# An encoder layer with 16 experts on one core: the Fourier transform and the ranks issued in steps, and gate and up in matmuls of 512 and 256 columns

## The chip, the core and the metric

The kernel runs on one core of a Trainium2 chip. A core has TensorE (matmuls; in the profile PE, its weight loads PEld), VectorE (DVE), ScalarE (ACT), GpSimd (POOL) and SyncE (SP, which here only issues DMAs). The metric is the device time of one execution in microseconds (us); the time before is the median of 3 runs.

## The reference, cut to what matters

One layer on a sequence of 2048 positions with 1024 channels, float32:

- `h = RMSNorm(x)`, `p = h @ w_in`, split into 512 columns each of `lru_x`, `lru_gate` and `fourier`.
- A = GeLU(lru_gate) * (forward + backward gated linear recurrence of a depthwise convolution of lru_x).
- B = the real part of a 2-D FFT over positions and channels of the `fourier` columns, in 4 groups of 128 channels.
- `x = x + concat[A, B] @ w_out`.
- A mixture of 16 experts: a softmax router gives every position a score for every expert; each expert takes its 256 best positions, gathers them, computes `silu(xin @ w_gate) * (xin @ w_up)` with 2048 hidden units, multiplies by `w_down`, scales by the score and adds the rows back. A last RMSNorm gives the output.

Every matmul of float32 operands is made of three in the format fp32r: each operand is split into a high part (a rounded copy, made on ScalarE) and a low part (the rest, made on VectorE), and the products high x high, high x low and low x high are added in PSUM. The helper `split` (L82, its instructions at L85 and L86) makes the parts, the helper `mm3` (L76, instructions L78, L79, L80) the three matmuls.

## The kernel before, in words

The instructions of one engine run in the order in which a planner has put them. The planner follows the order of the program and its own estimate of when each instruction could start; `issue_after` and `high_priority` move single ones. Tiles of one name share a fixed number of buffers; a buffer is given to the next tile when the last reader of the old one is done.

**Before the experts.** `pre_moe` (L176 to L497) computes the projections. `first_x` and `four` make lru_x for eight blocks of 256 positions. `lru(b)` (L280) computes the recurrence for 128 channels: convolution, 48 gate matmuls into PSUM tiles `gt`, sigmoids, tanh, exp, square, sqrt on ScalarE, and two scans of 2048 elements on VectorE (L328, L330). `mixin` and `stage1` make the Fourier columns and the first step of the transform, and store it in DRAM (`v_d`). `gates` makes lru_gate and stores it in DRAM (`gt_d`). lru(0) comes before the mixin loop, lru(1) in its block 4, lru(2) and lru(3) in blocks 0 and 4 of the gates loop (L369, L383). Then comes the transform (L477 to L491): 16 steps (i, gr), where `load_v` brings the columns back from DRAM and splits them into tiles `vl` (6 buffers), with the twiddle tiles `tw` (4), `stage2` multiplies them (PSUM `mm`) and splits the result into `xfh`/`xfl`, and `chans` of the step before multiplies by cosine and sine (PSUM `gt`) and adds into `Yt` (L470 to L475). In the same loop `gelu(i)` (L389) loads 2048 gate values per partition, applies GeLU and multiplies u, once in each i, and `load_wo` (L406) brings four of the eight row blocks of w_out; its low part is made on GpSimd (L412). The other four blocks are loaded after the transform.

**w_out and router.** `w_out_phase` (L503) handles 16 tiles of 128 positions: `prep(n)` splits u and Yt of a tile, `mix(n)` multiplies by w_out, first the four blocks of Yt, then the four of u, and the router follows some tiles later.

**Routing.** `routing` (L715): `first` finds the threshold of expert 0, `ranks` and `digits` turn scores above the threshold into slot numbers. For the other 15 experts `others` (L896) does the same in 30 steps of `search` on VectorE, followed at once by `ranks` (whose matmuls at L838 wait for its counts at L834 and L835), two transposes and `digits`. These steps are handed out by `aside` (L1162) while expert 0 is computed, three before and three after each `gate_up`.

**Experts.** `moe` (L911) loops over 16 experts of 8 chunks. A chunk holds 256 hidden units. `load(e, c)` fetches gate, up and down weights (1 MB each) into `raw`, and splits them into `wh` and `wl`, 4 buffers each. `gate_up(e, c)` (L1031) multiplies the gate weights, then the up weights: for each of two blocks `s` of 128 hidden units and each of 8 blocks `k` of channels one `mm3` with 256 columns, 96 matmuls in all. Then SiLU, product and split into `hh`. `down` of the chunk before follows, 24 matmuls of 512 columns. PSUM: three banks `mm`, four banks `dn`, one bank `gt`. In the program's order PE therefore runs gate_up(c), down(c-1), gate_up(c+1), down(c).

For the next expert `slots(e + 1)` is issued after `down` in chunk 3 (chunk 5 in expert 0): `pick` (L918) prepares `dv` on GpSimd, runs 16 small matmuls (L929), two more at L934 and one at L945 in the PSUM bank `gt`, VectorE derives the row numbers `iq` (L951), and GpSimd issues 8 gathers (L970). `xin(e + 1)`, issued in chunk 5 (chunk 7 in expert 0), transposes the gathered rows on VectorE (L994) and splits them into `xh` and `xl`.

Of the kernel before, what the change touches and what calls it, by code (L numbers as in the profile page):

```python
# [9 lines left out]
F32 = mybir.dt.float32  # L10
# [4 lines left out]
OP = mybir.AluOpType  # L15
# [131 lines left out]
def pre_moe(tc, nc, a, g, ctx):  # L147
# [115 lines left out]
    pg = tc.alloc_tile_pool(name="pg", bufs=1, reuse_waits="tile")  # L263
    with tc.tile_pool(name="pl", bufs=1, reuse_waits="tile") as pl:
        kk = pl.tile([P, 2, P], F32R, name="kk")
        split(nc, g.cc[:, 0:P], kk[:, 0], kk[:, 1])
# [13 lines left out]
        def lru(b):  # L280
# [11 lines left out]
            sg = [pg.tile([P, S], F32, name="rf", bufs=1), pg.tile([P, S], F32, name="if", bufs=1), t8("rb"), t8("ib")]  # L292
# [89 lines left out]
        for c in range(8):  # L382
            if c in (0, 4):  # L383
                load_gm(2 + c // 4)
                lru(2 + c // 4)
            if c + 1 < 8:
                pre[c + 1] = next_x(c + 1)
            gates(c, w, pre.pop(c))
    def gelu(b):  # L389
        gl = pg.tile([P, S], F32, name=("rf", "if")[b % 2], bufs=1)  # L390
        nc.sync.dma_start(gl.rearrange("p (c t) -> p c t", c=8), gt_d[:, b // 2, :, b % 2 * 256:b % 2 * 256 + 256].rearrange("c p t -> p c t"))
        with tc.issue_after(g.last_sqrt.ins):
            nc.scalar.activation(gl, gl, AF.Gelu_apprx_tanh)
        uv = u[:, b, 2:2 + S].rearrange("p (b t i) -> p t b i", t=16, i=8)
        V.tensor_tensor(uv, uv, gl.rearrange("p (t b i) -> p t b i", t=16, i=8), OP.mult)
# [10 lines left out]
    def load_wo(k, pool):  # L406
# [12 lines left out]
    def load_v(i):  # L419
        vv, tt = {}, {}  # L420
        with soon():
            for k2 in sets[i]:
# [4 lines left out]
                tt[k2] = tw
                for v in ([0] if k2 == 0 else [15] if k2 == 8 else [2 * k2 - 1, 2 * k2]):
                    raw = pf.tile([P, DL], F32, name="vraw", bufs=2)
                    nc.sync.dma_start(raw, g.v_d[v])  # L430
# [48 lines left out]
    for i in range(4):  # L479
        for gr in range(4):  # L480
# [12 lines left out]
    pg.release()  # L493
# [9 lines left out]
def w_out_phase(tc, nc, a, g):  # L503
# [26 lines left out]
    with tc.tile_pool(name="po", bufs=1, reuse_waits="tile") as po:  # L530
        wr = po.tile([P, KD, E], F32, name="wr")
# [685 lines left out]
```

## Time and profile before

| what | us |
|---|---|
| median of 3 runs (2901.05 to 2906.13) | 2905.11 |
| the profiled execution, its own time | 2904.78 |
| its span, first to last instruction | 2902.8 |
| TensorE busy in the span | 2817.6 (97%) |
| first gate_up matmul of expert 0 | 684.7 |
| first gate_up matmul of expert 1 | 825.3 |

Times in rows are microseconds from the start of the span. Matmuls are pipelined: the length that a row gives to one is its passage, and the distance between the starts of two is what it costs. PEclk is the granted TensorE clock, 1.00 for 2.4 GHz and 0.50 for 1.2 GHz.

### The profile page before, as it was taken

Reading aid. Unit: us, or ns where it says so; the run is one execution under the profiler, and the core shown is the slowest. Engines: PE = TensorE matmul, PEld = TensorE weight load, DVE = VectorE, ACT = ScalarE, POOL = GpSimd, SP = SyncE. Lnnn points to the kernel's source line nnn. Section 1 sums busy time; section 2 is a strip of 40 time slices with the busy share of each in tenths; the row PEclk is TensorE's granted clock in tenths of the full one; section 3 lists DMA queues with packets and bytes.
Section 4 is the critical chain, followed back from the end, with each engine's and each line's share of the span. In section 5 each row is a group of like instructions: output and inputs, shape, how many; then the busy total and the mean of one; then the engine's idle time right before and its main releaser. Section 6 shows DMA issues by size and latency. Waiting matters only on the chain.

```text
span 2902.8 us, 45048 instructions
## 1 busy us (share of the span) xinstructions
PE 2817.6 (97%) x19215; PEld 2596.3 (89%) x19215; DVE 1763.4 (61%) x2064; ACT 1282.1 (44%) x1341; POOL 412.3 (14%) x362
## 2 busy tenths in 40 slices
PE   8999979997999999999999999999999999999998
PEld 8878867776899999999999999999999999999997
DVE  7664775558865565555555555656555555565565
ACT  5584653333344334434343434434444434443465
POOL 3111122011021111111102020211111111111110
PEclk9999989997999999999999999999999999999999
DMA  8546454446565656565656566565656565656585
GB/s 298 198 162 204 170 190 146 155 149 227 174 206 202 200 192 203 197 197 202 202 192 203 198 193 210 187 212 204 202 191 203 197 198 200 203 191 202 200 290 221
DMA packets 129001, 578.45 MB, mean 199 GB/s; under 512 B 18176, under 2 KB 36000, under 8 KB 79648
## 3 DMA queue, kind: packets, MB, share of 16 engines
q1 hardware_dynamic: 108368, 507.37, 50.3%
q0 software_dynamic: 20288, 68.17, 8.2%
q8 instruction: 150, 2.46, 0.3%
q14 instruction: 51, 0.42, 0.0%
q10 hardware_dynamic: 144, 0.03, 0.0%
HBM read 508.40 MB, written 67.11 MB: 198 GB/s over the span
## 4 chain that ended last, share of the span: by engine, by line
PE 73%; DVE 2%; issue 0%; DMA 0%; ACT 0%; POOLq 0%; ACTq 0%
PE mm L78 17%; PE mm L79 16%; PE mm L80 16%; PE dn L78 8%; PE dn L79 8%; PE dn L80 8%; DVE wl L86 1%; DVE junk L793 0%; PE gt L929 0%; DVE cq L796 0%; DMA rows<-h_d,ix 0%; DVE cr L794 0%; DVE cs L795 0%; DMA out<-rows,ix 0%; DVE dl L826 0%
## 5 line engine op out<-in xcount | busy, mean ns | idle before, releaser
L85 ACT CAST wh<-raw 128x2048 fp32r<-128x2048 f32 x384 | 730.3, 1906 | 1190.2 <-PE mm L79 759.1
L86 DVE TENSOR_TENSOR wl<-raw,wh 128x2048 fp32r<-128x2048 f32 x384 | 888.8, 2318 | 562.4 <-ACT wh L85 561.3
L78 PE MATMUL mm<-xh,wh 128*128 128x256 f32 x4096 | 1163.0, 284 | 0.1
L79 PE MATMUL mm<-xl,wh 128*128 128x256 f32 x4096 | 1161.8, 284 | 0.3 <-DVE xl L86 0.3
L80 PE MATMUL mm<-xh,wl 128*128 128x256 f32 x4096 | 1160.3, 283 | 0.0
L78 PEld LDWEIGHTS mm<-xh,wh 128*128 128x128 f32 x4096 | 786.8, 192 | 7.5 <-ACT xh L85 0.3
L79 PEld LDWEIGHTS mm<-xl,wh 128*128 128x128 f32 x4096 | 786.8, 192 | 5.8 <-DVE xl L86 0.5
L80 PEld LDWEIGHTS mm<-xh,wl 128*128 128x128 f32 x4096 | 786.9, 192 | 4.6 <-issue 4.6
L78 PE MATMUL dn<-wh,hh 128*128 128x512 f32 x1024 | 400.0, 391 | 0.0
L79 PE MATMUL dn<-wl,hh 128*128 128x512 f32 x1024 | 399.9, 391 | 0.0
L80 PE MATMUL dn<-wh,hh 128*128 128x512 f32 x1024 | 398.3, 389 | 0.0
L80 PEld LDWEIGHTS dn<-wh,hh 128*128 128x128 f32 x1024 | 192.3, 188 | 40.9
L1072 POOL DMA_INDIRECT acc<-y,ix x30 | 70.9, 2362 | 1103.0 <-DVE y L1071 1020.9
L78 PEld LDWEIGHTS dn<-wh,hh 128*128 128x128 f32 x1024 | 192.8, 188 | 36.7
L79 PEld LDWEIGHTS dn<-wl,hh 128*128 128x128 f32 x1024 | 192.8, 188 | 35.1
L970 POOL DMA_INDIRECT rows<-h_d,iq x120 | 137.1, 1143 | 588.6 <-DVE iq L951 545.7
L1044 DVE TENSOR_TENSOR sg<-sg,mm 128x512 f32<-128x512 f32 x128 | 87.1, 681 | 151.4 <-PE mm L80 146.2
L78 PE MATMUL mm<-xx,w 128*128 128x256 f32 x512 | 147.2, 289 | 8.4 <-ACT xx L192 6.3
L994 DVE STREAM_TRANSPOSE z<-rows 128x256 f32<-128x256 f32 x120 | 74.3, 655 | 124.4 <-DMA rows<-h_d,iq 112.3
L79 PE MATMUL mm<-xx,w 128*128 128x256 f32 x512 | 146.5, 288 | 0.1
L80 PE MATMUL mm<-xx,w 128*128 128x256 f32 x512 | 145.3, 288 | 0.2 <-DVE w L89 0.2
L85 ACT CAST hh<-sg 128x512 fp32r<-128x512 f32 x128 | 78.6, 614 | 74.6 <-DVE sg L1044 74.5
(378 smaller groups left out, 2922.4 us busy)
## 6 DMA issues: line engine op xcount, KB each, us to landing
raw<-w_gate SPq DMA_DIRECT2D x128, 1024.0 KB, 4.9
raw<-w_up SPq DMA_DIRECT2D x128, 1024.0 KB, 4.8
raw<-w_down SPq DMA_DIRECT2D x128, 1024.0 KB, 4.9
xx<-x_d SPq DMA_DIRECT2D x64, 512.0 KB, 4.5
x_d<-xx SPq DMA_DIRECT2D x32, 512.0 KB, 3.8
xr<-xT SPq DMA_DIRECT2D x32, 256.0 KB, 4.0
xrow<-x SPq DMA_DIRECT2D x16, 512.0 KB, 3.7
acc<-x POOLq DMA_DIRECT2D x16, 512.0 KB
```

The lines of the kernel that those rows point to most:

```text
L78: nc.tensor.matmul(out, sh, mh, start=first, stop=False, skip_group_check=shared)
L79: nc.tensor.matmul(out, sh, ml, start=False, stop=False, skip_group_check=shared)
L80: return nc.tensor.matmul(out, sl, mh, start=False, stop=last, skip_group_check=shared)
L85: nc.scalar.copy(hi, raw)
L86: return nc.vector.tensor_tensor(lo, raw, hi.bitcast(F32), OP.subtract)
L970: nc.gpsimd.indirect_dma_start(out=r[:, o * 256:(o + 1) * 256], out_offset=None, in_=g.h_d.rearrange("t (q c) -> (t q) c", q=4), in_offset ...
L994: V.transpose(out=xt[:, :, 32 * o:32 * o + 32], in_=comb(rows[o // 4][:, o % 4 * 256:(o % 4 + 1) * 256]))
L1044: turn[e, c] = V.tensor_tensor(sg, sg, pu, OP.mult)
L1072: nc.gpsimd.indirect_dma_start(out=g.acc, out_offset=bass.IndirectOffsetOnAxis(ap=idx[h][:, :1], axis=0), in_=y, in_offset=None, compute_o ...
```

## The change

- The recurrences move forward: lru(1) and lru(2) to blocks 3 and 7 of the mixin loop, lru(3) to block 3 of the gates loop.
- `gelu` is cut in 16 pieces of 512 elements; its loads go from the SP queue to the GpSimd queue, 12 pieces are issued ahead of the transform, 4 within it. More buffers for `vraw`, `vl` (8) and `tw` (5); tiles are named at the head of each pool, which fixes their place in memory.
- The low part of w_out is made on VectorE instead of GpSimd. The blocks 0 to 3 (of u) are loaded during the transform, 4 to 7 (of Yt) after it. For the first two tiles the u half of `mix` is issued ahead of everything that reads Yt, into four PSUM banks `mm` that are kept until the Yt half has been added.
- `ranks` becomes a generator: after the counts, three steps pass before its matmuls, and three more before the transposes. `slots(1)` moves from chunk 5 to chunk 6 of expert 0.
- PSUM in the experts: four banks `mm`, four `dn`; `pick` takes one of the four `mm` banks.
- `xh` and `xl` become one tile, [k, high or low, 256]. From expert 1 on, for each block s and each of gate and up: eight matmuls of 512 columns (high weight times high and low input together), then eight of 256 (low weight times high input) into the first half of the bank. ScalarE copies the second half out, VectorE adds the first. SiLU, product and split run on 256 columns, per s.

```diff
-    pg = tc.alloc_tile_pool(name="pg", bufs=1, reuse_waits="tile")
     with tc.tile_pool(name="pl", bufs=1, reuse_waits="tile") as pl:
         kk = pl.tile([P, 2, P], F32R, name="kk")
+        for n, w_, b in (("f", 1024, 2), ("gm", 1024, 1), ("c", 1024, 3), ("ch", 1024, 2), ("rf", S, 1), ("if", S, 1), ("rb", S, 1), ("ib", S, 1),
+                         ("th", S, 2), ("v", 512, 4)):
+            pl.tile([P, w_], F32R if n in ("f", "gm", "ch") else F32, name=n, bufs=b)
...
         for c in range(8):
-            if c == 4:
-                load_gm(1)
-                lru(1)
+            if c in (3, 7):
+                load_gm(1 + c // 4)
+                lru(1 + c // 4)
...
         for c in range(8):
-            if c in (0, 4):
-                load_gm(2 + c // 4)
-                lru(2 + c // 4)
+            if c == 3:
+                load_gm(3)
+                lru(3)
...
-    def gelu(b):
-        gl = pg.tile([P, S], F32, name=("rf", "if")[b % 2], bufs=1)
-        nc.sync.dma_start(gl.rearrange("p (c t) -> p c t", c=8), gt_d[:, b // 2, :, b % 2 * 256:b % 2 * 256 + 256].rearrange("c p t -> p c t"))
+    def gelu(b, c):
+
+        gl = pf.tile([P, 512], F32, name="gl", bufs=4)
+        GP.dma_start(gl.rearrange("p (c t) -> p c t", c=2),
+                          gt_d[2 * c:2 * c + 2, b // 2, :, b % 2 * 256:b % 2 * 256 + 256].rearrange("c p t -> p c t"))
...
-        GP.tensor_tensor(g.wol[k], raw, g.woh[k].bitcast(F32), OP.subtract)
-
-    cs = pf.tile([P, 2, 2, P], F32R, name="cs")
+        V.tensor_tensor(g.wol[k], raw, g.woh[k].bitcast(F32), OP.subtract)
+
+    for n, w_, b in (("gl", 512, 4), ("vraw", DL, 3), ("traw", 384, 2), ("tw", 768, 5), ("cs", 512, 1), ("vl", 1024, 8)):
+        pf.tile([P, w_], F32R if n in ("cs", "tw", "vl") else F32, name=n, bufs=b)
+    back = [(b, c) for c in range(4) for b in range(4)]
+    for _ in range(12):
+        gelu(*back.pop(0))
...
             if gr == 2:
-                load_wo(4 + i, g.pw)
-            if gr == 3:
-                gelu(i)
+                load_wo(i, g.pw)
+            if back and i + gr:
+                gelu(*back.pop(0))
...
-    for k in range(4):
+    for k in range(4, 8):
         load_wo(k, g.pw2)
...
+        def mix_u(n):
+
+            mh, ml = mix_in[n]
+            for i in range(2):
+                p = begun[n, i] = ps.tile([P, 512], F32, name="mm", bufs=8 - g.ngt)
+                for k in range(4):
+                    mm3(nc, p, mh[:, k], ml[:, k], woh[k][:, i * 512:i * 512 + 512], wol[k][:, i * 512:i * 512 + 512], k == 0, False)
...
-                for j, k in enumerate((4, 5, 6, 7, 0, 1, 2, 3)):
-                    if i == 2 and j == 5:
+                k0 = 4 if n < 2 else 0
+                p = begun[n, i] if k0 else ps.tile([P, 512], F32, name="mm", bufs=8 - g.ngt)[:, :c1 - c0]
+                for k in range(k0, KD):
+                    if i == 2 and k == 5:
...
-        prep(0)
+        for n in range(2):
+            prep_u(n)
+            mix_u(n)
+        for n in range(2):
+            prep_y(n)
...
-    def ranks(sc, n, low, same):
+    def ranks(sc, n, low, same, pause=()):
...
         V.tensor_scalar(eq, sc, thr, None, op0=OP.is_equal, op1=OP.add, accum_out=cnt[:, 1:2])
+        yield from pause
...
-        pg = ranks(sc, 256, low, same)
+        yield from ranks(sc, 256, low, same, [None] * 3)
+        yield from [None] * 3
+        pg = g.pg
...
-            pp = ps.tile([P, 512], F32, name="gt", bufs=1)
+            pp = ps.tile([P, 512], F32, name="mm", bufs=4)
...
+            X[e] = x2 = mo.tile([P, KD, 2, CAP], F32R, name="xx", bufs=2)
+            xh, xl = x2[:, :, 0], x2[:, :, 1]
...
         def gate_up(e, c):
...
+            x2 = X[e]
+            xf = x2.rearrange("p k h t -> p k (h t)")
+            hh = mo.tile([P, 2, 512], F32R, name="hh", bufs=2)
+            if e == 0:
...
+            for s in range(2):
+                fs = slice(s * P, (s + 1) * P)
+                sg = mo.tile([P, 512], F32, name="sg", bufs=2)
+                gv, uv = sg[:, :CAP], sg[:, CAP:]
+                for m, v in enumerate((gv, uv)):
+
+                    p = ps.tile([P, 512], F32, name="mm", bufs=4)
+                    wh, wl = W[e, c][m]
                     for k in range(KD):
-                        mm3(nc, o, wh[:, k, fs], wl[:, k, fs], xh[:, k], xl[:, k], k == 0, k == KD - 1)
...
+                        nc.tensor.matmul(p, wh[:, k, fs], xf[:, k], start=k == 0, stop=False, skip_group_check=True)
+                    for k in range(KD):
+                        nc.tensor.matmul(p[:, :CAP], wl[:, k, fs], x2[:, k, 0], start=False, stop=k == KD - 1, skip_group_check=True)
+                    nc.scalar.copy(v, p[:, CAP:])
+                    V.tensor_tensor(v, p[:, :CAP], v, OP.add)
+                nc.scalar.activation(gv, gv, AF.Silu)
+                turn[e, c] = V.tensor_tensor(gv, gv, uv, OP.mult)
+                ss = slice(s * CAP, (s + 1) * CAP)
+                split(nc, gv, hh[:, 0, ss], hh[:, 1, ss])
             HH[e, c] = hh
...
-                    if c == (3 if e else 5):
+                    if c == (3 if e else 6):
                         with tc.issue_after(turn[e, c - 2].ins):
                             slots(e + 1)
```

## Rows read from the trace of the kernel before

**Rows 1.** The page: the busy time of the engines (share of the span, instructions), and the tenths of the granted clock in 40 equal slices of the span.
```profile
PE 2817.6 (97%) x19215; PEld 2596.3 (89%) x19215; DVE 1763.4 (61%) x2064; ACT 1282.1 (44%) x1341; POOL 412.3 (14%) x362
PEclk9999989997999999999999999999999999999999
```

**Rows 2.** Stretches of the span: from and to, length, then for PE, PEld, DVE, ACT and POOL the busy time and the instructions, the granted clock, the DMA share and GB/s.
```profile
367.00:438.00 71.00, 51.07 (x311) 45.40 (x309) 57.63 (x90) 42.39 (x73) 13.45 (x9) 0.86 0.55 181
842.00:2760.00 1918.00, 1918.00 (x13674) 1800.42 (x13673) 1107.36 (x949) 780.51 (x614) 257.57 (x168) 1.00 0.60 199
404.30:417.90 13.60, 9.58 (x42) 8.90 (x42) 9.75 (x14) 7.66 (x8) 0.00 (x0) 0.50 0.68 235
417.90:438.40 20.50, 16.07 (x102) 13.73 (x101) 18.76 (x39) 13.20 (x29) 1.77 (x1) 1.00 0.19 55
438.40:445.20 6.80, 4.02 (x9) 2.72 (x10) 6.80 (x10) 3.70 (x9) 4.40 (x3) 0.50 0.62 190
769.60:776.20 6.60, 6.06 (x31) 5.96 (x31) 6.06 (x13) 0.00 (x0) 0.00 (x0) 0.50 0.45 159
```

**Rows 3.** PE in order of time in a chunk of an expert (start, length, engine, line, operation): the first of 24 matmuls of down, the first of the 96 of gate_up after it, and the first of the next down.
```profile
1507.11 0.40 PE L78 MATMUL dn<-wh,hh 128*128 128x512 f32 x1
1512.57 0.28 PE L78 MATMUL mm<-xh,wh 128*128 128x256 f32 x1
1524.09 0.40 PE L78 MATMUL dn<-wh,hh 128*128 128x512 f32 x1
```

**Rows 4.** Groups of instructions on ScalarE and VectorE in the stretch 1495 to 1512.4, about one chunk: count, busy time, mean ns of one, idle time before them.
```profile
L86 DVE TENSOR_TENSOR wl<-raw,wh 128x2048 fp32r<-128x2048 f32 x3 | 6.9, 2293 | 7.1 <-ACT wh L85 7.1
L85 ACT CAST wh<-raw 128x2048 fp32r<-128x2048 f32 x3 | 5.7, 1906 | 10.2 <-PE mm L79 7.1 <-PE dn L80 3.2
L86 DVE TENSOR_TENSOR hh<-sg,hh 128x512 fp32r<-128x512 f32 x2 | 1.4, 686 | 0.0
L1044 DVE TENSOR_TENSOR sg<-sg,mm 128x512 f32<-128x512 f32 x1 | 0.7, 687 | 1.7 <-PE mm L80 1.7
```

**Rows 5.** Groups of instructions in the transform, VectorE in the stretch 369 to 437 and ScalarE in 367 to 437, in the columns of the group before.
```profile
L86 DVE TENSOR_TENSOR vl<-vraw,vl 128x512 fp32r<-128x512 f32 x16 | 15.1, 975 | 0.7 <-ACT vl L85 0.7
L86 DVE TENSOR_TENSOR tw<-traw,tw 128x384 fp32r<-128x384 f32 x9 | 8.6, 956 | 3.2 <-ACT tw L85 3.2
L470 DVE TENSOR_TENSOR Yt<-gt,bs 128x256 f32<-128x256 f32 x16 | 6.7, 418 | 1.4 <-ACT bs L467 1.3
L395 DVE TENSOR_TENSOR u<-u,rf 128x2048 f32<-128x2048 f32 x2 | 4.6, 2293 | 2.6 <-ACT rf L393 2.6
L467 ACT COPY bs<-gt 128x256 f32<-128x256 f32 x12 | 4.5, 373 | 5.0 <-PE gt L80 5.0
```

**Rows 6.** In order of time at the transform: VectorE and GpSimd where they run beside each other, a VectorE subtract of 1024 elements of the same kind, PE's first and last matmul of the transform, and PE's first of w_out. In brackets the engine's idle time before and what ended it.
```profile
371.15 5.95 DVE L86 TENSOR_TENSOR vl<-vraw,vl 128x512 fp32r<-128x512 f32 x2
371.29 4.65 POOL L412 TENSOR_TENSOR wol<-woraw,woh 128x1024 fp32r<-128x1024 f32 x2
288.91 1.22 DVE L304 TENSOR_TENSOR if<-if,c 128x1024 f32<-128x1024 f32 x1
369.54 0.28 PE L78 MATMUL mm<-tw,vl 128*128 128x256 f32 x1
435.06 0.34 PE L80 MATMUL gt<-xfh,cs 128*128 128x384 f32 x1
438.38 0.79 PE L78 MATMUL mm<-woh,mh 128*128 128x512 f32 x1 [2.98 <-ACT mh L85]
```

**Rows 7.** The waits of PE over the span: what waited, for what, us in total, times, longest.
```profile
PE mm L80 <- DVE vl L86: 8.2, 6, 4.8
PE mm L78 <- ACT vl L85: 6.9, 3, 3.2
PE gt L838 <- DVE gt__7210 L834: 4.6, 1, 4.6
PE mm L80 <- DVE ml L86: 2.8, 1, 2.8
```

**Rows 8.** In order of time, the input of expert 1: PE's first gate_up matmul after the small matmuls of `pick`, PE's next down, VectorE's first split into xl, and PE's first matmul of expert 1.
```profile
790.47 0.39 PE L78 MATMUL mm<-xh,wh 128*128 128x256 f32 x1
802.83 0.40 PE L78 MATMUL dn<-wh,hh 128*128 128x512 f32 x1
814.18 2.51 DVE L86 TENSOR_TENSOR xl<-z,xh 128x512 fp32r<-128x512 f32 x4
825.27 0.28 PE L78 MATMUL mm<-xh,wh 128*128 128x256 f32 x1
```

**Rows 9.** In order of time, chunks 4 and 5 of expert 4: PE's first gate_up matmul after `pick`, its first down, its first gate_up matmul of chunk 5, and VectorE's queue from the row numbers to the low part of the up weights of chunk 5.
```profile
1306.34 0.39 PE L78 MATMUL mm<-xh,wh 128*128 128x256 f32 x1
1318.70 0.40 PE L78 MATMUL dn<-wh,hh 128*128 128x512 f32 x1
1324.17 0.28 PE L78 MATMUL mm<-xh,wh 128*128 128x256 f32 x1
1316.67 1.22 DVE L994 STREAM_TRANSPOSE z<-rows 128x256 f32<-128x256 f32 x2 [5.44 <-DMA rows<-h_d,iq]
1325.38 1.22 DVE L994 STREAM_TRANSPOSE z<-rows 128x256 f32<-128x256 f32 x2 [3.59 <-DMA rows<-h_d,iq]
1327.68 2.25 DVE L86 TENSOR_TENSOR wl<-raw,wh 128x2048 fp32r<-128x2048 f32 x1
```

More of the change, by code (lines that the diff above doesn't have):

```diff
@@ L291, in lru @@
                     V.scalar_tensor_tensor(c, uu[:, n + k:m + k], g.cw[:, b, k:k + 1], c, op0=OP.mult, op1=OP.add)
-            sg = [pg.tile([P, S], F32, name="rf", bufs=1), pg.tile([P, S], F32, name="if", bufs=1), t8("rb"), t8("ib")]
+            sg = [t8(n) for n in ("rf", "if", "rb", "ib")]
             for j in range(4):
@@ L530, in w_out_phase @@
     with tc.tile_pool(name="po", bufs=1, reuse_waits="tile") as po:
+        po.tile([P, 512], F32, name="lg")
+        for n in ("mh", "ml"):
+            po.tile([P, KD, P], F32R, name=n, bufs=2)
         wr = po.tile([P, KD, E], F32, name="wr")
@@ L545, in w_out_phase, with prep_u @@
         nc.sync.dma_start(g2, a["g2"].to_broadcast([P, D]))
-        def prep(n):
+        def prep_u(n):
             mh = po.tile([P, KD, P], F32R, name="mh", bufs=2)
@@ L631, in unit @@
             if s:
-                lg = po.tile([2 * E, 256], F32, name="lg")
+                lg = po.tile([P, 512], F32, name="lg")[:2 * E, :256]
                 V.tensor_copy(lg, p[:2 * E, :256])
@@ L666, in router @@
                 return
-            lg = po.tile([2 * E, 256], F32, name="lg")
+            lg = po.tile([P, 512], F32, name="lg")[:2 * E, :256]
             V.tensor_copy(lg, q[:2 * E, :256])
@@ L893, in routing @@
     first(sc)
-    digits(ranks(sd, 16, before, ones), g.s1[:, 0], g.s0[:, 0], T([P, 256], "sq")[:, :16], T([P, 256], "pt")[:, :16])
+    for _ in ranks(sd, 16, before, ones):
+        pass
+    digits(g.pg, g.s1[:, 0], g.s0[:, 0], T([P, 256], "sq")[:, :16], T([P, 256], "pt")[:, :16])
     def others():
@@ L1029, in load, with half @@
             W[e, c] = r
+        def half(p, wh, wl, x2, fs):
+            for k in range(KD):
+                mm3(nc, p, wh[:, k, fs], wl[:, k, fs], x2[:, k, 0], x2[:, k, 1], k == 0, k == KD - 1)
         def gate_up(e, c):
[L1032 to L1041 removed]
@@ L1042, in gate_up @@
-            sg = mo.tile([P, 512], F32, name="sg", bufs=2)
-            nc.scalar.activation(sg, pg, AF.Silu)
-            turn[e, c] = V.tensor_tensor(sg, sg, pu, OP.mult)
-            hh = mo.tile([P, 2, 512], F32R, name="hh", bufs=2)
-            split(nc, sg, hh[:, 0], hh[:, 1])
+            x2 = X[e]
+            xf = x2.rearrange("p k h t -> p k (h t)")
+            hh = mo.tile([P, 2, 512], F32R, name="hh", bufs=2)
+            if e == 0:
+                ps_ = [ps.tile([P, 512], F32, name="mm", bufs=4) for _ in range(2)]
+                for m, p in enumerate(ps_):
+                    wh, wl = W[e, c][m]
+                    for s in range(2):
+                        half(p[:, s * 256:(s + 1) * 256], wh, wl, x2, slice(s * P, (s + 1) * P))
+                sg = mo.tile([P, 512], F32, name="sg", bufs=2)
+                nc.scalar.activation(sg, ps_[0], AF.Silu)
+                turn[e, c] = V.tensor_tensor(sg, sg, ps_[1], OP.mult)
+                split(nc, sg, hh[:, 0], hh[:, 1])
+                HH[e, c] = hh
+                return
@@ L1090, in final @@
             if not zb:
-                for t in ("xh", "xl"):
-                    zb.append(mo.tile([P, KD, CAP], F32R, name=t, bufs=2).rearrange("p (s k) t -> p s (k t)", s=2).bitcast(F32))
+                t = mo.tile([P, KD, 2, CAP], F32R, name="xx", bufs=2).rearrange("p (z s k) h t -> p z s (k h t)", z=2, s=2).bitcast(F32)
+                zb.extend([t[:, 0], t[:, 1]])
                 zb.append(mo.tile([P, 2, D], F32, name="z"))
@@ L1124, in moe @@
         NE = E
-        g.mm = g.gt = lambda: ps.tile([P, 512], F32, name="gt", bufs=1)
+        g.mm = g.gt = lambda: ps.tile([P, 512], F32, name="mm", bufs=4)
         slots(0)
```

46 lines of the change are left out of this document (21 added, 25 removed).

## The prediction

> **What bounds the kernel now.** I read the page first, then stretches of the span, PE's instructions in order of time, and PE's waits. TensorE is busy for 97% of the span and its clock is full in nearly all slices [rows 1]. In the experts, from 842 to 2760, it never idles and the clock is 1.00 [rows 2], while VectorE has 1107 and ScalarE 781 of 1918 us. There only what PE itself spends counts. PE does not spend by columns alone: 24 matmuls of down take 1512.57 - 1507.11 = 5.46 us, 227 ns each; 96 of gate_up take 1524.09 - 1512.57 = 11.52 us, 120 ns each [rows 3]. Twice the columns cost 107 ns more, so about 13.3 ns of every matmul depend on its number and not on its width.
>
> The other place where time can be had is the transform: between 367 and 438 PE is busy for 51 of 71 us at a mean clock of 0.86, with VectorE at 57.6 [rows 2]; PE waits there for the split columns `vl` [rows 7]. A single wait of 4.6 us is that of the rank matmuls [rows 7].
>
> **Gate and up, -51.1 us.** 96 matmuls of 256 become 32 of 512 and 32 of 256, the same columns with 32 matmuls less: 32 x 13.3 = 0.426 us a chunk, 11.52 to 11.09. It holds for 15 experts x 8 chunks = 120: 51.1 us, all on the path, since PE never waits there. The trace has both widths in fp32r on this engine, so the bounds are narrow, 50 to 53. By the Trainium skill, "TensorE: Matmul & The Clock Gate", section Back-to-back issue gap, a matmul costs its columns over 2.4 GHz and only about 2.5 ns more; by that this sum would be some 10 us. The trace has 13.3, and I take the trace.
>
> What it adds lies beside PE. ScalarE copies 4 x 128x256 out of PSUM a chunk, 0.37 us each as bs<-gt has; VectorE adds 4, 0.42 each as Yt<-gt,bs has [rows 5]. SiLU, product and split run on twice as many instructions of half the length, at most some 0.15 us more for each pair. Over the experts ScalarE has 781/1918 of 16.98 us, 6.9 a chunk, and VectorE 9.8 [rows 2]; they rise to 8.7 and 11.8 of a chunk of 11.09 + 5.46 = 16.55 us, the weight splits, 5.7 and 6.9, included [rows 4]. A bank `mm` is refilled a whole chunk later, or, while `pick` holds one of the four, after two other quarter chunks, 5.5 us: a copy behind one `wh` (1.9) and an add behind one `wl` (2.3) make 5.0. I cost it at nothing; without this cover PE would wait for a bank.
>
> **Weights come free later, needed earlier; +11 us.** With s outermost, gate's buffer is free after three quarters of gate_up instead of half, and up's is wanted after a quarter instead of half. In an ordinary chunk gate's low part had from 5.76 us into one chunk to 0.24 into the next, 11.5 us, and now has from 8.32 to 1.81, 10.0 us; its split takes 1.9 + 2.3 [rows 4]. It is tight in one chunk of each expert, chunk 5, where VectorE's queue stands in front of the gathered rows: it waits 5.4 and 3.6 us for them, and the up weights of that chunk are split only behind the last transpose, 1327.68 + 2.25 = 1329.93, 23.6 us after `pick` [rows 9]. PE wants the low part at 1324.17 + 48 x 0.12 + 0.24 = 1330.17, so nothing is left over. In the new order PE comes to chunk 5 at 11.09 + 0.86 (the share of `pick`, from 1318.70 - 1306.34 = 12.36) + 5.46 = 17.4 us after `pick`, and to up's low part a block and eight wide matmuls later, 2.77 + 1.81: at 22.0. The gathers hang on `pick`, not on PE's pace, so it is 1.6 us late. If the planner puts this split ahead of the last transposes, because the buffer is free earlier, it is not late at all. The order is not in this trace; I take half, 0.8 x 14 experts = 11 us, with bounds 0 and 28 (2 us each, the short extra VectorE work in the queue included).
>
> **Ranks, -7.6 us; the input of expert 1, +9 us.** Three steps later the counts are long there: the 4.6 us go, and so does the half-clock stretch after it, 6.06 us of work at 0.50 [rows 2], worth 3.0. What is late next: `digits` comes in step 37, so `slots(1)` moves behind chunk 6. `pick` ended at 790.47 and the first part of `xl` was there at 814.18 + 0.7 = 814.9, 24.4 us later; expert 1 began 34.8 us after `pick` [rows 8]. A chunk later only 12.36 + 5.46 = 17.8 us remain: gate_up(1, 0), and in PE's queue all behind it, down(0, 7) first, waits 6.6 us, and with another half-clock stretch (3.0) loses 9.6. I take 9; the bounds are 0 (the planner puts down(0, 7) ahead, 5.5 us, and VectorE, by then free of the search, is quicker) and 10.
>
> **Transform, -20 us, and the start of w_out, -5 us.** PE's own work there is 16 steps of 12 and 12 of 6 matmuls of 256 columns, and 24 matmuls of 384, 31.7 + 24 x 0.173 = 35.8 us, but they span 369.54 to 435.06 + 0.3, 66 us [rows 6]. VectorE has the most to do, 57.6 us [rows 2]. Of that goes: the slowing by GpSimd, two `vl` taking 5.95 beside two `wol` [rows 6]; against 686 ns for 128x512 in the experts, and three quarters of that for 384 [rows 4], it is (975 - 686) x 16 + (956 - 515) x 9 ns = 8.6 us [rows 5]; 12 of 16 pieces of gelu, 6.9 of 9.2; and, with lru(3) some 12 us or more earlier and room for two sets of `vl` and `tw`, about 7.7 of splits, before the last gates matmul ends. Four `wol` on VectorE add 4 x 1.22 = 4.9 [rows 6]. 57.6 - 1.4 (two last pieces of gates) - 8.6 - 6.9 - 7.7 + 4.9 = 38, with the router's weights and `prep_u` some 42. At the share VectorE had in 417.90 to 438.40, 0.915 [rows 2], that is 46 us instead of 66. The 48 matmuls of `mix_u` (48 x 0.227 = 10.9 us, no new work) then fill PE where Yt is still awaited: of the waits of 2.98 [rows 6] and 2.8 [rows 7] and the half clock of 438.40 to 445.20 [rows 2] I count 5 us as gone. The bounds are -38 (PE's 35.8 us alone, no waits, no half clock) and 0: four banks `mm` of five are held by `mix_u` while the last steps need two each, so what is won can be given back. The 16 gelu loads now stand in GpSimd's queue between the gates' stores and the recurrences' last adds, and each waits for one of four buffers; a store held up there would hold a tile `v` of the gates, of which there are four. The SP queue is rid of four loads of 1 MB. I cost both at nothing. The recurrences keep PE's work, and each still waits for the buffers of the one before; I cost the move at 0, between -5 and +5.
>
> **The sum.** 2904.8 (the profiled execution; the median is 0.3 above, its span 2.0 below) - 51.1 - 25 - 7.6 + 9 + 11 = **2841.1 us**.
>
> **The rivals.**
> - No late weights, and expert 1's input in time: 2904.8 - 51.1 - 25 - 7.6 = 2821. For it speaks the earlier buffer, against it that PE followed the program's order at `pick`. Chance 0.12.
> - The transform is bound by VectorE as before and its work only moves: 2841 + 25 = 2866. For it speaks VectorE's 57.6 of 71 us [rows 2], against it the part that only GpSimd caused. Chance 0.12.
> - The gain by matmul number is not there for gate_up: at 2.5 ns each only 9.6 us, 2841 + 41.5 = 2883. Against it stand 120 and 227 ns [rows 3]. The page's formula, above, says this. Chance 0.04.
> - **Slower:** chunk 5 of each expert stalls long enough for the clock to fall. Waits of 2.98 and 4.6 us were followed by stretches at 0.50 [rows 2, 6, 7] which cost about 3 us. A stall of 3.4 us, the 1.6 above and 1.8 of queued adds and splits, and 3.0 of clock, 14 times, are 90 us instead of 11: 2841 - 11 + 90 = 2920. It decides from (51.1 + 25 + 7.6 - 9) / 14 = 5.3 us an expert. Against it: VectorE waits 9 us for rows in this stretch anyway, which takes up the adds. The same page's section on a second HAM failure mode says that cycling through PSUM banks can let the clock swing; the trace cycles through seven banks at a clock of 1.00 [rows 2]. Chance 0.08, of which 0.03 end within 0.2%.
>
> **How the numbers follow.** The forecast has 0.64. Its own bounds reach from 2904.8 - 51.1 - 38 - 7.6 - 5 = 2803 to 2841 + 25 + 17 + 6 = 2889. For 8 in 10 I leave out the last few at either end: 2808 to 2876. Runs of this kernel differ by some 0.2%, 5.8 us, about what a measurement can tell from no change. Slower by more: 0.05; within: 0.04; faster: 0.91.
>
> **What would show it.** Right: gate_up from expert 1 on takes 11.1 us, wide matmuls start 227 ns apart; no wait at the ranks, one of several us at the first gate_up of expert 1; chunk 5 of each expert with a PE wait of 0 to 2 us for `wl`; the transform about 46 us long, no GpSimd subtract beside it. Wrong: wide matmuls at 240 ns (the same columns would then cost no less), PE waits in every chunk, or a transform still over 60 us.

## The result: 2859.7 us against 2904.7 us, 18.6 us above the forecast

The changed kernel takes 2859.66 us (median of 4 runs, 2856.60 to 2862.61), the kernel before 2904.73 on the same chip: ratio 0.9839, 95% interval 0.9827 to 0.9851. The forecast was 2841.1, range 2808 to 2876. The profiled execution of the changed kernel, called after below, has a span of 2855.92 us. Cut at the same matmuls as the trace of before (us of span):

| stretch | before | after | profiles of equal code there |
|---|---|---|---|
| start to the last gates matmul | 369.4 | 363.3 | before 369.9; after 365.5 to 368.5 |
| to the first w_out matmul (transform) | 69.0 | 69.4 | before 69.5; after 69.0 to 71.6 |
| to the first gate_up | 246.3 | 241.9 | before 247.0; after 241.6 to 242.3 |
| to the start of the last matmul (experts) | 2206.1 | 2165.2 | |
| to the end | 12.0 | 16.0 | |

The last column has six experiments below that leave everything ahead of the experts as in after, and one that leaves it as before: the first stretch differs by 5 us between executions of the same code, so the 6.1 us of the two profiles are some 3.2 in the mean (366.4 against 369.7). The transform gave nothing, the experts 40.9, and the end grew by 4.0, for which the prediction had no term.

The page of after, its engine totals and granted clock, answers to [rows 1]:

```profile
PE 2768.2 (97%) x15375; PEld 2388.3 (84%) x15375; DVE 1950.1 (68%) x2804; ACT 1487.7 (52%) x2073; POOL 353.5 (12%) x370
...
PEclk9999989997999999999999999999999999999999
```

That is 3840 matmuls less, 120 chunks by 32; the busy time of VectorE and ScalarE rose by 187 and 206 us. The stretches of after, in the columns of [rows 2]: ahead of the transform, the transform, the experts.

```profile
340.00:363.60 23.60, 23.60 (x197) 23.41 (x196) 3.33 (x5) 3.79 (x4) 5.86 (x8) 1.00 0.61 211
363.60:432.70 69.10, 48.09 (x289) 44.53 (x288) 54.04 (x106) 41.26 (x82) 12.43 (x18) 0.80 0.54 184
842.00:2710.00 1868.00, 1868.00 (x10039) 1599.41 (x10038) 1274.20 (x1609) 968.06 (x1278) 207.62 (x167) 1.00 0.59 203
```

In the experts PE has no idle time and the full clock, as before; in the transform VectorE still works 54.0 us. PE in order of time in a chunk of after, beside [rows 3]:

```profile
1506.75 0.39 PE L80 MATMUL dn<-wh,hh 128*128 128x512 f32 x1
1506.98 1.98 PE L1095 MATMUL mm<-xx,wh 128*128 128x512 f32 x8
1508.79 1.12 PE L1097 MATMUL mm<-xx,wl 128*128 128x256 f32 x8
1509.74 2.00 PE L1095 MATMUL mm<-xx,wh 128*128 128x512 f32 x8
1511.59 1.11 PE L1097 MATMUL mm<-xx,wl 128*128 128x256 f32 x8
...
1518.12 0.40 PE L78 MATMUL dn<-wh,hh 128*128 128x512 f32 x1
...
1523.59 1.98 PE L1095 MATMUL mm<-xx,wh 128*128 128x512 f32 x8
```

Read the differences of the starts: eight narrow matmuls take 0.95 us (119 ns each); eight wide ones 1.81 behind down, but 1.85 behind narrow ones. gate_up takes 11.14 us (1506.98 to 1518.12) instead of 11.52, a chunk 16.61 instead of 16.98, an expert 134.60 instead of 137.46. The costliest waits of PE over the span of after, beside [rows 7]:

```profile
PE mm L78 <- ACT vl L85: 10.5, 3, 7.9
PE mm L1095 <- DVE xx L86: 6.2, 1, 6.2
```

The rank wait is gone, the input of expert 1 (`xx`) waits 6.2 in its place, and one wait of 7.9 stands ahead of the transform. From 690 us on, the wait for `xx` is the only one that PE has; for late weights there is no row at all.

### The profile page after: what moved, and what is told of

Same layout as the page of the kernel before. It is cut to its first block, busy times and chain, and to the rows that moved or that the text cites. A ratio compares the mean times of both kernels' runs of the same rounds, so it can differ in the third digit from the quotient of the medians.

```text
span 2855.9 us, 39182 instructions
## 1 busy us (share of the span) xinstructions
PE 2768.2 (97%) x15375; PEld 2388.3 (84%) x15375; DVE 1950.1 (68%) x2804; ACT 1487.7 (52%) x2073; POOL 353.5 (12%) x370
## 4 chain that ended last, share of the span: by engine, by line
PE 71%; issue 4%; DMA 1%; POOL 0%; DVE 0%; ACT 0%; POOLq 0%; SPq 0%
PE mm L1095 30%; PE mm L1097 15%; PE dn L78 8%; PE dn L79 8%; PE dn L80 8%; PE mm L79 1%; PE mm L78 1%; PE mm L80 1%; PE mm L964 0%; DMA rows<-h_d,iq 0%; DMA acc<-y,ix 0%; DMA rows<-h_d,ix 0%; DMA xx<-acc 0%; POOL out L1163 0%; DMA out<-xx 0%
## 5 line engine op out<-in xcount | busy, mean ns | idle before, releaser
L1095 PE MATMUL mm<-xx,wh 128*128 128x512 f32 x3840 | 970.2, 393 | 6.2 <-DVE xx L86 6.2
L1095 PEld LDWEIGHTS mm<-xx,wh 128*128 128x128 f32 x3840 | 696.1, 189 | 137.5 <-issue 6.6
L1097 PEld LDWEIGHTS mm<-xx,wl 128*128 128x128 f32 x3840 | 524.4, 191 | 37.7
L1097 PE MATMUL mm<-xx,wl 128*128 128x256 f32 x3840 | 535.8, 282 | 0.0
L85 ACT CAST hh<-sg 128x256 fp32r<-128x256 f32 (+1 forms) x248 | 102.5, 413 | 431.1 <-DVE sg L1101 417.3
L1099 DVE TENSOR_TENSOR sg<-mm,sg 128x256 f32<-128x256 f32 x480 | 200.3, 418 | 142.4 <-ACT sg L1098 142.4
L1098 ACT COPY sg<-mm 128x256 f32<-128x256 f32 x480 | 175.3, 366 | 163.4 <-PE mm L1097 163.4
L80 PEld LDWEIGHTS dn<-wh,hh 128*128 128x128 f32 x1024 | 192.3, 188 | 40.9
L1100 ACT ACTIVATE sg<-sg 128x256 f32<-128x256 f32 x240 | 100.4, 418 | 223.4 <-DVE sg L1099 170.9
L1129 POOL DMA_INDIRECT acc<-y,ix x30 | 48.0, 1601 | 1050.6 <-DVE y L1128 970.4
L86 DVE TENSOR_TENSOR hh<-sg,hh 128x256 fp32r<-128x256 f32 (+1 forms) x248 | 106.2, 428 | 76.0 <-ACT hh L85 75.8
```

Of the source, the lines that this page charges most:

```text
L80: return nc.tensor.matmul(out, sl, mh, start=False, stop=last, skip_group_check=shared)
L85: nc.scalar.copy(hi, raw)
L86: return nc.vector.tensor_tensor(lo, raw, hi.bitcast(F32), OP.subtract)
L1095: nc.tensor.matmul(p, wh[:, k, fs], xf[:, k], start=k == 0, stop=False, skip_group_check=True)
L1097: nc.tensor.matmul(p[:, :CAP], wl[:, k, fs], x2[:, k, 0], start=False, stop=k == KD - 1, skip_group_check=True)
L1098: nc.scalar.copy(v, p[:, CAP:])
```

## The experiments

Every ratio is to the kernel before on the same chip; the changed kernel stands at 0.9839 [0.9827, 0.9851]. Only e1_gu256 and e13_all lie clear of that interval. What the other runs show is read from the stretches of one profile each. In the five profiles that leave the expert loop as in after, the experts take 2163.8 to 2165.2 us; the difference lies in expert 0, and each expert after it takes 134.60 us in all of them.

**Gate and up, undone and alone.** e1_gu256 takes the old matmuls for all experts:

```diff
-            if e == 0:
+            if e >= 0:
```

> The changed kernel with gate and up as 96 matmuls of 256 columns in every expert (input layout and four banks kept). Theory: a matmul costs about 13.3 ns beyond its columns, so the eight-wide form is worth the 0.37 us a chunk that the two traces differ by, 120 chunks: back comes 44 us, to about 2904, and the end of the kernel, which grew from 12.0 to 16.0 us after the last matmul, shrinks again with fewer ScalarE and VectorE instructions: 2900. Rival A (2.5 ns a matmul): 32 x 2.5 ns x 120 = 10 us back, 2870. Rival B (the gain came from the new layout or the fourth bank, not from the width): 2860, no change.

Measured: 2900.76 us, ratio 0.9974 [0.9964, 0.9984]; experts 2206.7 us, +41.5, an expert 137.46 again, end 13.6. e5_only_gu is the mirror: the kernel before with the diff's `xin`, `half`, `gate_up`, `zb` and the four banks `mm`, nothing else.

> The kernel before with nothing but the new gate and up from the second expert on (joined input tile, four banks in one pool). Theory: 0.37 us for each of 120 chunks, -44 us, and some +4 us at the end, where ScalarE and VectorE have more to do: ratio 0.986, about 2865 against 2905; expert 1 has no wait, since the slots stay after chunk 5. The mirror of this, the changed kernel with 256 columns, came out 41 us above the changed kernel. Rival (part of the 44 us is owed to the other edits): less than 35 us gained.

Measured: 2864.93 us, ratio 0.9861 [0.9846, 0.9876]; experts 2162.3, -43.7, an expert 134.60, end 14.5. Both say the same: the new form of gate and up alone is worth 41 to 44 us of the 45 in the experts, and part of the longer end belongs to it. That the new input layout or the fourth bank made the gain is ruled out, since e1_gu256 keeps both.

**Does the switch of width cost?** e8_order runs both wide blocks of a half first:

```diff
+                ps_ = [ps.tile([P, 512], F32, name="mm", bufs=4) for _ in range(2)]
+                for m, p in enumerate(ps_):
+                    for k in range(KD):
+                        nc.tensor.matmul(p, W[e, c][m][0][:, k, fs], xf[:, k], start=k == 0, stop=False, skip_group_check=True)
                 for m, v in enumerate((gv, uv)):
-
-                    p = ps.tile([P, 512], F32, name="mm", bufs=4)
-                    wh, wl = W[e, c][m]
-                    for k in range(KD):
-                        nc.tensor.matmul(p, wh[:, k, fs], xf[:, k], start=k == 0, stop=False, skip_group_check=True)
+                    p, wl = ps_[m], W[e, c][m][1]
                     for k in range(KD):
```

> The changed kernel with each half of gate and up as 16 matmuls of 512, gate's then up's, and 16 of 256 behind them. In the changed kernel eight wide matmuls take 1.84 us where they follow narrow ones and 1.81 where they follow down, and the chunk is 0.05 us longer than its matmul prices add up to. Theory (the switch between widths costs some 0.03 us): two switches less a chunk, 0.06 x 120 = -7 us, ratio 0.9815. Rival (the count of matmuls alone counts, switches cost nothing): 0.9839; it could be slower if the high part of the up weights, wanted after 1.8 instead of 2.8 us, is late in chunk 5.

Measured: 2861.69 us, ratio 0.9844 [0.9831, 0.9858], no gain in the total. Its PE in order of time:

```profile
1507.24 0.39 PE L80 MATMUL dn<-wh,hh 128*128 128x512 f32 x1
1507.46 3.79 PE L1093 MATMUL mm<-xx,wh 128*128 128x512 f32 x16
1511.09 2.08 PE L1097 MATMUL mm<-xx,wl 128*128 128x256 f32 x16
1513.00 0.40 PE L1093 MATMUL mm<-xx,wh 128*128 128x512 f32 x1
```

Sixteen wide ones take 3.63 us, 227 ns each, so the switch does cost: an expert takes 134.31 us, 0.29 less, which is 4.4 us over 15 of them; the experts' stretch is 5.2 shorter. The end took 2.8 of it back (18.8 us).

**Ranks and the input of expert 1.** e2_nosteps takes the pauses out and puts `slots` back behind chunk 5:

```diff
-        yield from ranks(sc, 256, low, same, [None] * 3)
-        yield from [None] * 3
+        yield from ranks(sc, 256, low, same)
...
-                    if c == (3 if e else 6):
+                    if c == (3 if e else 5):
```

> The changed kernel without the pauses at the ranks, and with the slots of expert 1 after chunk 5 again. Theory (the two cancel): the rank matmuls wait 4.6 us again and 3 us of half clock follow, +7.6; the wait of 6.2 us at the first gate_up of expert 1 and its 2.7 us of half clock go, -8.9: about 2858, the same within 0.2%. Rival (the wait at expert 1 has another cause, the joined input tile): it stays, and the rank wait comes on top, 2867.

Measured: 2857.98 us, ratio 0.9829 [0.9816, 0.9842]. PE's waits from 690 us on are those of the search's steps again, now mostly at a down that needs `hh` from VectorE, and the one at expert 1 is gone:

```profile
PE dn L80 <- DVE hh L86: 2.8, 1, 2.8
PE mm L869 <- DVE gt__7272 L864: 0.7, 1, 0.7
PE dn L78 <- ACT hh L85: 0.4, 1, 0.4
```

With 3.1 of half clock (6.16 us of work at 0.50) that is 7.0 us. In after, PE in order of time at expert 1, and the stretch behind it:

```profile
814.70 1.62 PE L1095 MATMUL mm<-xx,wh 128*128 128x512 f32 x3 [6.23 <-DVE xx L86]
```

```profile
813.50:820.30 6.80, 5.60 (x16) 4.68 (x17) 5.06 (x6) 1.69 (x1) 0.00 (x0) 0.50 0.52 175
```

6.23 and 2.8 of half clock (5.60 us of work at 0.50), 9.0. By this the steps cost 2.0 us net, and the experts take 2165.2 against 2163.3. Against the other four profiles with after's expert loop it is 0.5 to 1.8, so the steps gain nothing, and that they cost anything is not clear of the spread. e6_ranks tried to have both, with three more steps of the search behind the down of chunk 5 and `slots` there:

```diff
                     down(*pend)
+                    if c == 5:
+                        aside(e, 3)
...
-                    if c == (3 if e else 6):
+                    if c == (3 if e else 5):
```

> The changed kernel with three more steps of the search taken behind the down block of chunk 5, so that the digits are ready and slots of expert 1 follow in chunk 5 again; the pause ahead of the rank matmuls stays. Theory: both waits go, that of the ranks (2.8 to 4.6 us and a half-clock stretch) and that at the first gate_up of expert 1 (6.2 us and 2.7 of clock): -9 us, ratio 0.9808 against 0.9839. Rival (the transposes for the digits now wait for VectorE inside chunk 5, or the slots come too late all the same): at most -4.

Measured: 2863.64 us, ratio 0.9853 [0.9838, 0.9868], a miss. PE's waits in expert 0:

```profile
PE mm L964 <- POOL dv L960: 2.9, 2, 2.5
PE mm L80 <- DVE wl L86: 1.8, 1, 1.8
PE mm L78 <- ACT wh L85: 1.8, 1, 1.8
```

Expert 1 is in time, but `pick` waits for GpSimd's product and two weight splits come late behind the new work. Two half-clock stretches followed, and the experts take 2167.5.

**The transform.** In after, GpSimd issues the first gelu loads behind the last store of the gates, ScalarE's first gelu waits for them, and the copies to `vl` that PE needs stand behind this gelu:

```profile
364.64 0.54 POOL L363 DMA_DIRECT2D gt_d<-v  x1 [0.18 <-issue]
365.17 2.87 POOL L394 DMA_DIRECT2D gl<-gt_d  x4
...
370.35 0.63 ACT L397 ACTIVATE gl<-gl 128x512 f32<-128x512 f32 x1 [6.80 <-DMA gl<-gt_d]
```

e3_vfirst and e9_vfirst2 order the gelu activations behind the first set of `vl`; only the second, tied to ScalarE's own copy, changed its order.

```diff
-        with tc.issue_after(g.last_sqrt.ins):
+        with tc.issue_after(g.last_vl.ins):
             nc.scalar.activation(gl, gl, AF.Gelu_apprx_tanh)
...
-    for _ in range(12):
-        gelu(*back.pop(0))
...
     load_v(0)
+    for _ in range(12):
+        gelu(*back.pop(0))
```

> The changed kernel with the first set of transform inputs ahead of the twelve gelu pieces in the program and the gelu activations ordered behind its last split. Theory: TensorE's 7.9 us before the transform are ScalarE's copies of vl standing behind the first gelu, which waits for a load issued behind the last gates store; they go, and part of the half clock after them (10.2 us at half clock cost 5): -8 to -12 in the transform's start; VectorE and ScalarE then still have the gelu pieces to do inside the transform, which may give back some. About 2850. Rival (the splits of vl wait for their own loads or tiles): no change, 2860; or the gelu pieces only move the wait to later steps: 2860.

Measured: 2861.06 us, ratio 0.9838 [0.9825, 0.9852], ScalarE's order and the wait (8.1 us) as they were: it tells nothing of the theory.

> As e3_vfirst, whose order on ScalarE stayed as it was and which therefore tested nothing; here the twelve gelu activations are ordered behind ScalarE's own copies of the first set of vl, and these stand ahead of the first gelu in its queue. Theory: the 7.9 us wait ahead of the transform goes, with part of the 10.2 us at half clock behind it (5 us lost): -8 to -12, ratio 0.980, if the gelu work fits into the transform; rival: VectorE and ScalarE owe the same work before the end of the transform, the wait only moves into later steps: between 0 and -3, ratio 0.983 to 0.984.

Measured: 2861.56 us, ratio 0.9841 [0.9828, 0.9854]. The first wait fell to 3.5 us, but nine more followed in the steps behind it (seven in after), 16.6 us in all against 18.3, and the transform took 69.8: the rival held. e11_gelsp goes at the loads:

```diff
-        GP.dma_start(gl.rearrange("p (c t) -> p c t", c=2),
+        (nc.sync if c < 3 else GP).dma_start(gl.rearrange("p (c t) -> p c t", c=2),
...
     for _ in range(12):
-        gelu(*back.pop(0))
+        with soon():
+            gelu(*back.pop(0))
```

> The changed kernel with the first twelve gelu loads on SyncE's queue, ahead of the loads of the transform's inputs, instead of on GpSimd's queue behind the last gates store; nothing left out. From the end of the gates to the first matmul of w_out it is 69.0 us before the change and 69.4 after it, with 54 us of VectorE work in it; in the 23.6 us before that VectorE works 3.3. Theory: the gelu pieces were meant for that idle time and did not get there because their loads were issued at 365 us; from SyncE they run before the gates end, VectorE's 54 us lose 7 and the first wait of 7.9 us goes too: 69 falls to 55 to 60 us, -9 to -14, ratio 0.9795. Rival A (the transform's own chain from TensorE over ScalarE and VectorE back sets its length): the wait at the start moves into its steps, 66 to 69 us, ratio 0.983. Rival B: the loads hold up SyncE's queue and the gates with it, slower.

Measured: 2859.77 us, ratio 0.9840 [0.9826, 0.9853], transform 68.0. ScalarE in order of time shows why:

```profile
358.90 1.05 ACT L415 CAST woh<-woraw 128x1024 fp32r<-128x1024 f32 x1 [18.05 <-PE mm L80]
366.10 1.05 ACT L415 CAST woh<-woraw 128x1024 fp32r<-128x1024 f32 x1 [6.15 <-PE mm L80]
367.16 1.28 ACT L397 ACT_TABLE_LOAD   x1
368.46 2.19 ACT L397 ACTIVATE gl<-gl 128x512 f32<-128x512 f32 x4
```

Two copies for w_out, whose place the gates still use, stand at the head of the queue, and four gelu pieces behind them. After has the same two at 353.58 and 360.78. e12_woh adds to e11_gelsp (`g.last_vl` is ScalarE's last copy of the first set):

```diff
-        nc.scalar.copy(g.woh[k], raw)
+        with tc.issue_after(g.last_vl.ins):
+            nc.scalar.copy(g.woh[k], raw)
```

> e11_gelsp, and the copies of w_out's first rows (woh) ordered behind the first set of vl on ScalarE. In e11_gelsp four gelu pieces had their data some 8 us before ScalarE took them up at 368.46: its queue stood at two woh copies, which waited 18.05 and 6.15 us for the gates' matmuls, because woh lies where the gates' inputs lie. Theory: this head-of-line wait on ScalarE is what keeps the early work out of the idle time ahead of the transform; with it gone the gelu pieces and the first vl run before the gates end, and the 68 to 69 us from the end of the gates to the first w_out matmul become 55 to 60: -9 to -13, ratio 0.980. Rival (the loop from TensorE over ScalarE and VectorE back sets the length of the transform whatever comes early): 65 us or more, ratio 0.983 or above.

Measured: 2856.55 us, ratio 0.9822 [0.9808, 0.9835], transform 66.3. ScalarE, then VectorE, in order of time:

```profile
359.75 1.36 ACT L397 ACTIVATE gl<-gl 128x512 f32<-128x512 f32 x2 [18.24 <-DMA gl<-gt_d]
361.31 0.63 ACT L397 ACTIVATE gl<-gl 128x512 f32<-128x512 f32 x1 [0.20 <-DMA gl<-gt_d]
362.84 0.63 ACT L397 ACTIVATE gl<-gl 128x512 f32<-128x512 f32 x1 [0.90 <-DMA gl<-gt_d]
```

```profile
356.10 1.41 DVE L361 TENSOR_TENSOR v<-mm,R 128x512 f32<-128x512 f32 x2 [10.11 <-PE mm L80]
367.62 1.41 DVE L361 TENSOR_TENSOR v<-mm,R 128x512 f32<-128x512 f32 x2 [10.11 <-PE mm L80]
...
369.28 2.49 DVE L399 TENSOR_TENSOR u<-u,gl 128x512 f32<-128x512 f32 x4
```

ScalarE now works ahead of the gates' end, but the products on VectorE stand behind the gates' last evacuation, with 10 us of idle time in front of it. Three queues were each held by one instruction that waits for the gates; with two freed, 3 of the 9 to 13 us came, less than its theory wanted; 66.3 lies on the rival's side. VectorE's work in the transform stayed at 54.4 us. A change of VectorE's order was not tried, so how much of the rest is the transform's own loop stays open. A third limit that no run tested is the loading. The transform of after, in the columns of [rows 2]:

```profile
371.50:382.00 10.50, 9.56 (x54) 8.85 (x54) 9.29 (x16) 8.96 (x17) 3.54 (x5) 0.76 1.03 360
382.00:392.00 10.00, 6.04 (x26) 5.24 (x26) 7.76 (x14) 7.73 (x15) 3.27 (x5) 0.66 0.96 333
```

Here the DMA share is 1.03 and 0.96 at 360 and 333 GB/s, against 0.54 over the whole transform: the loads of the gate values, the columns and w_out crowd in its first 20 us, in which PE's clock is 0.76 and 0.66. How much of the waits is owed to them is not shown.

**The end.** e4_junk writes the squares of `final` into tile `y`, instead of `sg`, which gate_up holds twice a chunk:

```diff
-                junk = mo.tile([P, 512], F32, name="sg", bufs=2)
+                junk = mo.tile([P, D], F32, name="y", bufs=2)[:, :512]
```

> The changed kernel with the squares of the last rows written into tile y instead of into sg, which gate_up now holds twice a chunk. Theory: the final blocks' squares waited for an sg buffer in the last chunk, so the last out store is 2.3 us later against the last matmul and the scatters behind it too; with a tile of their own the end shrinks from 16.0 to some 13 us: 2857. Rival (ScalarE's order, not the tile, sets it): 16 us stay, 2860.

Measured: 2868.27 us, ratio 0.9862 [0.9847, 0.9877], slower than the 2857 expected. The end fell to 14.6, but free of `sg` the squares ran ahead of a weight copy in expert 15, as PE's wait shows:

```profile
2760.22 3.78 PE L1095 MATMUL mm<-xx,wh 128*128 128x512 f32 x8 [3.62 <-ACT wh L85]
```

With the half clock behind this wait the last expert takes 7.3 us more than in after.

e10_tail takes the final blocks earlier:

```diff
                 elif c >= 1:
-                    final(c - 1)
-        final(7)
+                    for n in ((0,), (1, 2))[c - 1] if c < 3 else (c,):
+                        final(n)
```

> The changed kernel with the final blocks one chunk earlier (two in chunk 2, the last in chunk 7), nothing else. Theory: the end after the last matmul, 16.0 us against 12.0 before the change, hangs on the store of the last final block, which the scatters into the same output wait for; it was issued 0.0 us before the last matmul's start against 2.3 before the change. With this store a chunk (16.6 us) earlier the end falls to 11 to 12 us: -4 to -5, ratio 0.9824. Rival (the end is set by VectorE's and ScalarE's own work on the last rows): 15 to 16 us stay, 0.9839. If the squares now stand ahead of a weight split, as in e4_junk, a wait of TensorE of 3 to 4 us in expert 15 takes it back.

Measured: 2857.11 us, ratio 0.9834 [0.9820, 0.9847]; the end is 13.4 us, 2.6 less, and no wait came. GpSimd's issues at the end, of before (last matmul 2890.76), of after (2839.88) and of e10_tail (2841.94):

```profile
2888.43 0.70 POOL L1106 DMA_DIRECT2D out<-xl  x1 [2.41 <-DVE xl L1084]
2893.71 1.00 POOL L1121 DMA_INDIRECT out<-rows,ix  x1 [4.58 <-DVE fs L1118]
2897.86 1.00 POOL L1121 DMA_INDIRECT out<-rows,ix  x1 [3.15 <-DMA out<-rows,ix]
```

```profile
2839.87 0.70 POOL L1163 DMA_DIRECT2D out<-xx  x1 [2.87 <-DVE xx L1141]
2845.30 1.03 POOL L1178 DMA_INDIRECT out<-rows,ix  x1 [4.73 <-DMA out<-xx]
2849.48 1.00 POOL L1178 DMA_INDIRECT out<-rows,ix  x1 [3.15 <-DMA out<-rows,ix]
```

```profile
2838.13 0.70 POOL L1163 DMA_DIRECT2D out<-xx  x1 [12.37 <-DVE xx L1141]
2844.79 1.00 POOL L1178 DMA_INDIRECT out<-rows,ix  x1 [5.97 <-DVE fs L1175]
2848.94 1.00 POOL L1178 DMA_INDIRECT out<-rows,ix  x1 [3.15 <-DMA out<-rows,ix]
```

In after the first scatter starts 5.4 us behind the last matmul's start and is held by the last block's store; in e10_tail 2.9, as before the change, held by VectorE again. The store was the cause of 2.6 of the 4.0 us. The other 1.4 lie behind the second scatter: from its start to the end of the span it is 4.9 us before, 6.4 in after and in e10_tail. In e11_gelsp and e12_woh, whose end has the code of after, it is 5.1. So this part is not tied to the new gate and up, and what sets it is open.

**Together.** e13_all joins e12_woh, e10_tail, e2_nosteps and e8_order.

> The edits that shortened their own stretch, together: e12_woh (transform 69.4 to 66.3 us), e10_tail (end 16.0 to 13.4), e2_nosteps (first gate_up to last matmul 2165.2 to 2163.3) and e8_order (2165.2 to 2160.0, but an end of 18.8). Theory (the stretches add, and with the last final block a chunk earlier the long end of e8_order does not come back): -3 -2.6 -2 -4.5, some 12 us below the changed kernel, ratio 0.980. Rival (what is won in one stretch is lost in the next, as the end in e8_order and the waits at expert 1 did): ratio 0.982 or above.

Measured: 2850.24 us, ratio 0.9800 [0.9787, 0.9813], below after's interval: the best version, some 0.4% below the changed kernel. Its profile is its slowest run (2858.58), with 372.9 us up to the last gates matmul where e12_woh had 368.0; behind that it has experts 2160.9, end 13.6, transform 67.2. By stretch that is -4.3, -2.4 and -2.2 against after, 8.9 of the some 12 us expected: about three quarters of the gains add. In the experts e2_nosteps and e8_order gave 4.3 together and 2.0 and 5.2 alone (a wait of 1.1 us for `wl` in expert 15 is new).

## Why the prediction was right in sign and range, and where it failed

- **Gate and up, -51.1: right in mechanism, 42.9 measured** (15 x 2.86 us; undone it costs 41.5, alone it brings 43.7), outside the bounds of 50 to 53 that this term was given. The price by matmul number holds, but the sum used too large a one: [rows 3] give 2 x 120 - 227.5 = 12.5 ns a matmul, not 13.3, and 48 us instead of 51. A chunk would then take 16.58 us and takes 16.61, some 4 us over 120 chunks: the wide matmuls behind narrow ones cost more (1.85 against 1.81 for eight), which e8_order confirms with 16.57. The last 1 us is the chunk with `pick`, which became shorter by 0.29 us and not by 0.37. By the Trainium skill, "TensorE: Matmul & The Clock Gate", section Back-to-back issue gap, the gap of an isolated matmul is its columns over 2.4 GHz and about 2.5 ns, which would have given 10 us here; no run agrees with that, and the section itself says that in a stream of weight loads and matmuls, as this kernel is, both set the spacing.
- **Late weights, +11: 0 measured.** The case named beside it came: the split stands ahead of the last transposes. VectorE in chunks 4 and 5 of expert 4, beside [rows 9]:

```profile
1301.73 0.68 DVE L1028 STREAM_TRANSPOSE z<-rows 128x256 f32<-128x256 f32 x1 [0.50 <-DMA rows<-h_d,iq]
...
1305.42 2.26 DVE L86 TENSOR_TENSOR wl<-raw,wh 128x2048 fp32r<-128x2048 f32 x1
...
1310.14 0.67 DVE L1028 STREAM_TRANSPOSE z<-rows 128x256 f32<-128x256 f32 x1 [1.24 <-DMA rows<-h_d,iq]
```

  It ends at 1307.7; PE wants the low part of up at 1310.5. The extra copies and adds, costed at nothing, cost nothing up to the last expert.
- **Ranks -7.6 and input of expert 1 +9: right**, 7.0 and 9.0. Each was sized by its own wait and the half clock behind it, and they nearly cancel.
- **Transform, -20: 0 measured. This is the step that failed.** It let 6.9 us of gelu and 7.7 of splits leave VectorE's stretch because VectorE is idle before it. VectorE's groups in the transform of after, 363.6 to 432.7, beside [rows 5]:

```profile
L86 DVE TENSOR_TENSOR vl<-vraw,vl 128x512 fp32r<-128x512 f32 x16 | 10.5, 688 | 4.4 <-ACT vl L85 4.4
L399 DVE TENSOR_TENSOR u<-u,gl 128x512 f32<-128x512 f32 x16 | 10.5, 687 | 4.6 <-ACT gl L397 4.6
L416 DVE TENSOR_TENSOR wol<-woraw,woh 128x1024 fp32r<-128x1024 f32 x6 | 7.2, 1221 | 0.4 <-ACT woh L415 0.2
```

  The slowing by GpSimd went (688 ns instead of 975), six `wol` came, and all 16 products of gelu and all 16 splits of `vl` are still inside, so VectorE has 54.0 us there and not some 42. The second factor failed too: 0.915 was VectorE's share in one good stretch, and over the transform of after it is 54.0 of 69.1, 0.78. The prediction itself had named a transform of over 60 us as a sign of being wrong. The loads stood behind GpSimd's last gates store, ScalarE's queue behind two woh copies, VectorE's behind the gates' evacuation (e9, e11, e12). The prediction named GpSimd's queue only for what the loads would hold up, and costed it at nothing, not for what holds up the loads. With the wait of 7.9 us and the half clock behind it, VectorE's 3.6 us less showed nowhere either.
- **Start of w_out, -5: 4.4 here, 4.9 in the mean**, though `mix_u` did not fill the transform's tail: it starts behind it, at 432.74, after a wait of 2.67.
- **Recurrences, 0 between -5 and +5: -3.2 in the mean**, within the spread of this stretch.
- **The end, not costed: +4.0.** The cover named for ScalarE and VectorE in a chunk does not hold in the last one, where the final blocks' squares share both engines and tile `sg`.

Errors against the forecast: +8 gate and up, -11 weights, +20 transform, -3 recurrences, +4 end, about +1 for the rest: the 18.6 us. That the time lies in the range is in part luck, since the weights that did not come late paid for half of the transform that did not get shorter. The rival of the transform that only moves, 2866, came nearer than the forecast; the rival without late weights had its first half right.

## What to carry to other kernels

Price a matmul by two widths of the same trace and take both the slope and the constant; fewer, wider matmuls paid 43 us here with the same columns. Idle time on an engine is no room for work unless the work's place in that queue, and in the queues of its load and of its other half, is ahead of the instruction that waits: look for the head of each queue. A change in a loop's body has to be costed once more in the last iteration, where other work shares its cover.

## What the runs showed of the hardware

- Eight matmuls of 512 columns take 1.81 us behind others of 512, and 1.84 to 1.85 behind ones of 256.
- e1_gu256's record gives the clock as 0.95 where the others give 1.00, at the same matmul times (a chunk is 16.98 us there as in the kernel before), and no higher figure stands in its record; so 0.95 is taken as the full level there:

```profile
842.00:2400.00 1558.00, 1557.84 (x11090) 1461.84 (x11089) 898.13 (x765) 633.64 (x498) 211.54 (x135) 0.95 0.61 199
```

- Equal code ahead of the experts ends its gates between 363.3 and 368.5 us; what sets this was not found, and one pair of profiles can hide some 5 us there.
